# Up projection of a ConvGLU layer: token combinations of the second half made early and kept in DRAM, and boundary pairs in a new product order

## The chip, the cores and the metric

The kernel runs on one core of one Trainium2 chip. The metric is device time in microseconds (us), the median of several runs.

## The reference

One layer of a hybrid encoder in float32, 2048 tokens of width 1024. After an attention and mLSTM mixer come the two lines that this change touches:

```
def conv_glu_ffn(h, w_gate, conv_w, conv_b, w_up, w_down):
    a = dwconv_centred(h @ w_gate, conv_w, conv_b)
    return (jax.nn.gelu(a, approximate=False) * (h @ w_up)) @ w_down
...
        h = rmsnorm(x, ln_ffn_g[i])
        x = x + conv_glu_ffn(h, w_ffn_gate[i], ffn_conv_w[i], ffn_conv_b[i], w_ffn_up[i], w_ffn_down[i])
```

The hidden width is 2816, so gate and up together are 2048 x 1024 by 1024 x 5632. The convolution has width 3 over the tokens.

## The kernel before, in words

**Products.** Both projections run as Strassen's algorithm on 2 x 2 blocks: seven products instead of eight, each of a combination of two weight blocks with a combination of two token blocks. Every operand is split into a high part of reduced precision (`h`, made by ScalarE's copy) and the rest (`l`, made by VectorE's subtraction), and a product is the sum of three matmuls (h h, h l, l h). With four steps of 128 along the contraction, one product of one pair is a block of 12 matmuls of 128 x 512 (lines L1811, L1812, L1813 in `matmuls`). `PRODUCTS[j]` names the weight blocks and the token blocks of product j. Products 2 and 5 use one token block as it is, the other five a sum or difference of two.

**Order.** `FfnUp` takes two passes s, one for each half of the tokens (1024). In a pass it goes through 11 pairs i of 128-feature tiles, in a pair first the gate (m = 0), then up (m = 1), and in each the seven products in `ORDER` = (1, 2, 5, 3, 4, 6, 7). That is 2 x 11 x 2 x 7 = 308 blocks, 3696 matmuls. The blocks stand in one loop over n. Block n also calls for the weight combination of block n + 3 (`AHEAD_W`; tiles `fw`, from `fraw`, L175 and L176), for the weight load of a later group (`prefetch`), and for what is due behind the finished products: `outputs` moves banks of PSUM into `ext` (gate) and `up` (L1830 copies on ScalarE, L1833 additions on VectorE), `convolve` and `product` make the result, which goes to `a_d` in DRAM. GpSimd takes some of the weight sums and the last multiplication.

**Token combinations.** The seven pairs `bh`, `bl` of a half (2 x 1 MB each) stay in memory during the whole pass, 14 of the 22 pages of the pool that all large tiles share. `tokens(s)` loads the four blocks of the half from the transposed input `xT_d` (`bx`, 1 MB each, SP's queue) and makes them, step by step. For the first half the generator `early` lets four steps run in the last steps of the mix output (`MixOut`, the stage before, one token tile of 128 in each step t), which yields products 1, 2 and 5; the other four come during the first gate. For the second half all of it happens in the up blocks of the last pair of the first pass and the blocks behind: when product j has been used for the last time, its pages go back (`del self.b[j]`) and the next step of `tokens(1)` runs.

**Ends.** Behind the last step of MixOut stands the last tile's normalisation (`xn`, L1658), its eight transposes on TensorE and the store of `xT` to `xT_d` (L1737, ScalarE's queue); `next(between)` places the transposes and the store at block 2. `begin` clears the borders of `ext` (L1854, L1855), which uses slots of the small pool `raw` (four) that also holds `xT`, `xn` and early sums. At the other end, during the up blocks of the last pair, `next(after)` runs steps of `FfnDown.first`, which makes the first weights (`wd`, from `dr`) of the down projection and its first token sums (`as`, `al`, in `combine`, from `ar`); its matmuls are lines L147 to L149. `combine` takes the `al` tile from `slot`, a ring of four of which the first loads hold some.

Of the kernel before, what the change touches and what calls it, by code (L numbers as in the profile page):

```python
# [1755 lines left out]
class FfnUp(Strassen):  # L1756
# [5 lines left out]

    def __init__(self, g, pool):
# [7 lines left out]
        self.w, self.raws = {}, {}  # L1771
        self.blocks = [(s, i, m, j) for s in range(2) for i in range(NF // 2) for m in range(2) for j in ORDER]
# [13 lines left out]
    def weights(self, n):  # L1786
# [3 lines left out]
        if n % 7 == 0:  # L1790
            self.r = self.raws.pop(n // 7)
# [4 lines left out]
        def blk(x):  # L1796
            return None if x is None else self.r[:, 4 * x[1]:4 * x[1] + 4, P * x[0]:P * x[0] + P]

        one, two, sign = PRODUCTS[j][0]
        total = None if two is None else self.total([P, 4, P], n < NRAW)  # L1800
        split_sum(g, [nc.gpsimd if on_pool(j, e) else nc.vector for e in range(2)], w[:, 0], w[:, 1], blk(one), blk(two), sign, total)
        self.w[n] = w
        if n % 7 == 6:
            self.r = None
# [9 lines left out]

    def prefetch(self, q):

        if q < len(self.blocks) // 7:
            s, i, m, _ = self.blocks[7 * q]
            self.raws[q] = self.load_w(i, m)

    def run(self, between, after, tokens):
# [3 lines left out]
        st = Ctx()  # L1825

        def outputs(bank, dst):
# [7 lines left out]
            (c11, c12), (c21, c22) = dst  # L1835
            return {
# [55 lines left out]

        for n in range(AHEAD_W):
            if n not in self.w:
                self.weights(n)
        acts = {}
        for n in range(N + 1):
            if n < N:
                s, i, m, j = self.blocks[n]
                if j == 1:  # L1900
                    bank = {}
                    ext = up = dst = steps = None
                    dst = begin(s, i, m)
                    steps = outputs(bank, dst)
                    self.prefetch(n // 7 + 2)
# [24 lines left out]
            if j in steps:  # L1930
                todo.append(steps[j])
# [406 lines left out]
```

## Time and profile before

| what | value |
| --- | --- |
| median of 3 runs | 3026.34 us (3025.4 to 3026.8) |
| the profiled execution, own time | 3035.82 us |
| its span | 3034.1 us |
| mean granted TensorE clock over the span | 0.959 |
| up projection in the trace | about 1421 to 2345 us |
| pass boundary | about 1877 us |

Times in the trace are microseconds from the start of the span. Engines are PE (matmul), PEld (weight load), DVE (VectorE), ACT (ScalarE), POOL (GpSimd) and SP (the queue of most DMAs). A line `A <- B: x, n, y` of a waits view says that instructions of A stood idle x us in all, n times, the longest y, until B released them.

### The profile page before, as it was taken

The page shows a single profiled execution, that of the slowest core. Times are in us where ns is not written, and L with a number is a line of the kernel's source. Part 1 is how long each engine was busy: PE and PEld are TensorE (multiplying, and loading weights), DVE is VectorE, ACT ScalarE, POOL GpSimd, SP SyncE. Part 2 cuts the span into 40 slices and gives each one's busy share as a digit, 9 for nine tenths or more (in the row PEclk, how much of TensorE's full clock was granted, in tenths as well). Part 3 has the DMA queues.
Part 4 walks back from the last instruction along what each step waited for, and adds up shares of the span by engine and source line. Part 5 has one row for each costly group of instructions (what it writes and reads, how often), then busy time and mean ns, then how long its engine had stood idle before and what let it go on. Part 6 is the DMA issues. An engine that isn't in the chain of part 4 may idle for free. (4 is left out here: it accounts for less than half of the span.)

```text
span 3034.1 us, 40809 instructions
## 1 busy us (share of the span) xinstructions
PE 2867.8 (95%) x14474; PEld 2438.3 (80%) x14474; DVE 2039.0 (67%) x4107; ACT 1277.5 (42%) x2428; POOL 1090.6 (36%) x1146
## 2 busy tenths in 40 slices
PE   8898899889999988998899999799999999999999
PEld 7877888689999877787688887688887788888887
DVE  5866796675565578435977777977777576655444
ACT  5555465424333346323444444444444332233332
POOL 2133422415554555101433333433334251452221
PEclk9999999888899999999899999899999999999999
DMA  7744425466453473666122223222224877674111
GB/s 216 213 139 132 137 88 169 120 156 132 106 128 76 145 238 120 164 208 197 58 82 84 84 84 112 69 84 84 84 83 130 301 283 245 241 258 153 44 44 44
DMA packets 378731, 419.75 MB, mean 138 GB/s; under 512 B 106560, under 2 KB 299968, under 8 KB 372880
## 3 DMA queue, kind: packets, MB, share of 16 engines
q1 hardware_dynamic: 333920, 379.40, 40.7%
q10 hardware_dynamic: 44608, 37.76, 4.0%
q8 instruction: 114, 1.87, 0.3%
q14 instruction: 89, 0.73, 0.1%
HBM read 308.16 MB, written 104.61 MB: 136 GB/s over the span
## 5 line engine op out<-in xcount | busy, mean ns | idle before, releaser
L1811 PE MATMUL ps<-bh,fw 128*128 128x512 f32 x1232 | 495.6, 403 | 33.1 <-ACT fw L176 11.4
L1813 PE MATMUL ps<-bh,fw 128*128 128x512 f32 x1232 | 491.7, 399 | 6.8 <-DVE fw L176 6.8
L1812 PE MATMUL ps<-bl,fw 128*128 128x512 f32 x1232 | 492.6, 400 | 5.6 <-DVE bl L176 3.0
L175 POOL TENSOR_TENSOR sum<-fraw 128x512 f32<-128x512 f32 x132 | 197.3, 1496 | 404.4 <-DVE fw L176 364.4
L1811 PEld LDWEIGHTS ps<-bh,fw 128*128 128x128 f32 x1232 | 236.2, 192 | 97.6 <-ACT fw L176 13.6
L1813 PEld LDWEIGHTS ps<-bh,fw 128*128 128x128 f32 x1232 | 236.0, 192 | 64.0 <-DVE fw L176 9.5
L1812 PEld LDWEIGHTS ps<-bl,fw 128*128 128x128 f32 x1232 | 236.5, 192 | 61.6 <-DVE bl L176 6.2
L148 PE MATMUL ps<-wd,as 128*128 128x512 f32 x616 | 243.3, 395 | 0.0
L147 PE MATMUL ps<-wd,as 128*128 128x512 f32 x616 | 243.2, 395 | 0.0
L176 ACT ACTIVATE fw<-sum 128x512 fp32r<-128x512 f32 x220 | 134.7, 628 | 243.1 <-DVE sum L175 142.6
L176 DVE TENSOR_TENSOR fw<-sum,fw 128x512 fp32r<-128x512 f32 x220 | 214.6, 990 | 12.0 <-ACT fw L176 11.8
L996 ACT ACTIVATE e<-psb 128x512 f32<-128x512 f32 (+2 forms) x240 | 95.6, 437 | 217.9 <-PE psb L992 206.6
L930 POOL TENSOR_SCALAR_AFFINE_SELECT e<-e 128x64 f32<-128x64 f32 (+2 forms) x225 | 103.2, 459 | 203.6 <-ACT e L996 201.9
L1884 POOL TENSOR_TENSOR act<-act,up 128x512 f32<-128x512 f32 x88 | 128.9, 1465 | 93.7 <-DVE up L1833 73.3
L958 DVE CUSTOM_DVE_ANT_0 junk<-psa,mask 128x256 bf16<-128x256 f32 (+1 forms) x304 | 111.5, 367 | 73.4 <-PE psa L950 64.4
L176 ACT ACTIVATE as<-ar 128x640 fp32r<-128x640 f32 x112 | 84.2, 785 | 160.5 <-POOL ar L175 67.1
L1875 DVE SCALAR_TENSOR_TENSOR act<-ext,fcw,act 128x512 f32<-128x512 f32 (+1 forms) x176 | 138.6, 826 | 16.7 <-ACT act L1873 15.3
L175 POOL TENSOR_TENSOR ar<-ar 128x640 f32<-128x640 f32 x40 | 72.7, 1817 | 204.7 <-DMA ar<-a_d 195.2
L147 PE MATMUL ps<-wv,bh 128*128 128x260 f32 x448 | 131.3, 293 | 9.8 <-DVE acc L439 8.4
L149 PE MATMUL ps<-wd,al 128*128 128x512 f32 x336 | 133.1, 396 | 5.6 <-DVE al L176 5.6
L147 PEld LDWEIGHTS ps<-wd,as 128*128 128x128 f32 x616 | 116.2, 189 | 27.4
L148 PEld LDWEIGHTS ps<-wd,as 128*128 128x128 f32 x616 | 116.3, 189 | 27.2
(361 smaller groups left out, 7910.5 us busy)
## 6 DMA issues: line engine op xcount, KB each, us to landing
ar<-a_d SPq DMA_DIRECT2D x56, 704.0 KB
wdr<-in_w_ffn_down_dram SPq DMA_DIRECT2D x50, 512.0 KB
fraw<-in_w_ffn_gate_dram SPq DMA_DIRECT2D x22, 1024.0 KB
fraw<-in_w_ffn_up_dram SPq DMA_DIRECT2D x22, 1024.0 KB
a_d<-act SPq DMA_DIRECT2D x88, 256.0 KB
xT_d<-xT ACTq DMA_DIRECT2D x32, 512.0 KB
bx<-xT_d SPq DMA_DIRECT2D x16, 1024.0 KB
ab<-a_d SPq DMA_DIRECT2D x40, 384.0 KB
```

The source lines that it names most:

```text
L147: g.nc.tensor.matmul(out, lhsT=sh, rhs=mh, start=start, stop=False)
L148: g.nc.tensor.matmul(out, lhsT=sh, rhs=ml, start=False, stop=False)
L149: g.nc.tensor.matmul(out, lhsT=sl, rhs=mh, start=False, stop=stop)
L175: eng[0].tensor_tensor(src, a, b, ALU.add if sign > 0 else ALU.subtract)
L176: return (lambda: g.nc.scalar.activation(hi, src, AF.Copy)), (lambda: eng[1].tensor_tensor(lo, src, hi.bitcast(F32), ALU.subtract))
L930: nc.gpsimd.affine_select(l, l, pat + [[s, half - off]], ALU.is_ge, 0.0, base=s * off + w, channel_multiplier=-1)
L958: nc.vector.tensor_tensor_reduce(shape3(p, junk[:, :n], lo, hi), o, m, 1.0, -3e38, ALU.add, ALU.max, mst[:, p, i:i + 1])
L1811: nc.tensor.matmul(ps, lhsT=w[:, 0, k], rhs=h[:, k], start=start and k == 0, stop=False, skip_group_check=True)
L1812: nc.tensor.matmul(ps, lhsT=w[:, 0, k], rhs=l[:, k], start=False, stop=False, skip_group_check=True)
L1813: nc.tensor.matmul(ps, lhsT=w[:, 1, k], rhs=h[:, k], start=False, stop=k == 3, skip_group_check=True)
L1875: nc.vector.scalar_tensor_tensor(act, ext[a][:, lo + k:hi + k], self.cw[:, k, f:f + 1], act, ALU.mult, ALU.add)
L1884: nc.gpsimd.tensor_tensor(act, act, up[a][:, lo:hi], ALU.mult)
```

## The change

- `ahead` makes the combinations of products 1, 5, 4 and 7 of the first half in the last steps of MixOut, all on VectorE, from loads of 512 KB (`bq`). `rest` makes 3, 2 and 6 in the first pair, from three loads `bx`.
- The first and the last pair of each pass (`BOTH`) run the order `ORDER2`, and alternate gate and up for each product, so that a combination is used by two blocks in a row. Their outputs are moved in another order (`PAIRED`, and a second table in `outputs`; not shown below).
- `spill` makes all seven combinations of the second half during pairs 1 to 9 of the first pass, one k of four at a time: a load `sx` of 1 MB, 12 sums and differences of VectorE and 7 copies of ScalarE, and four stores of `sp` to a new DRAM tensor `b_d`. It is one call on every second block, 13 calls for one k.
- `fetch` loads the finished combinations from `b_d` into `bh` and `bl`, two loads of 1 MB for each product, when the pages of the first half come free. `tokens(1)` is gone.
- `next(after)` is still called in the up blocks of the last pair, which now alternate with the gate's. `combine` takes a page for the `al` tile of the down projection's first three items.

```
+    ORDER2 = (1, 5, 4, 7, 3, 2, 6)
+    BOTH = ((0, 0), (0, NF // 2 - 1), (1, 0), (1, NF // 2 - 1))
+    COME = (0, 2, 3, 4, 5, 6, 7, 8)
+    LOADS = (7, 9)
...
+        self.groups = [(s, i, m) for s in range(2) for i in range(NF // 2) for m in range(2)]
+        self.blocks = []
+        for s in range(2):
+            for i in range(NF // 2):
+                pair = [(s, i, m, j) for m in range(2) for j in ORDER]
+                self.blocks += sorted(pair, key=lambda b: self.ORDER2.index(b[3])) if (s, i) in self.BOTH else pair
...
+    def ahead(self):
+        g, nc = self.g, self.g.nc
+        parts = [(j, k) for j in self.ORDER2[:4] for k in (0, 2)]
...
+            r = page(g, [P, 2, 2, 512], F32, name="bq")
+            for q, blk in enumerate((one, two)):
+                if blk is not None:
+                    nc.sync.dma_start(r[:, q], self.block(0, *blk, k, 2))
+            raws.append(r)
...
+        for n, (j, k) in enumerate(parts):
+            two, sign = PRODUCTS[j][1][1:]
+            r = raws.pop(0)
+            h, l = self.pages(j) if k == 0 else self.b[j]
+            for q in range(2):
+                a = r[:, 0, q]
+                split_sum(g, (nc.vector, nc.vector), h[:, k + q], l[:, k + q], a, None if two is None else r[:, 1, q], sign, a)
+            r = None
+            if n + 2 < len(parts):
+                load(*parts[n + 2])
+            yield
...
+    def rest(self):
+        g, nc = self.g, self.g.nc
+        blocks = {}
+        def load(*blk):
+            blocks[blk] = page(g, [P, 4, 512], F32, name="bx")
+            nc.sync.dma_start(blocks[blk], self.block(0, *blk))
...
+        load(0, 1)
+        load(1, 1)
+        yield
+        load(0, 0)
+        yield
+        yield from make(3)
+        blocks.pop((1, 1))
+        yield from make(2)
+        yield from make(6)
...
+    def spill(self):
+        g, nc = self.g, self.g.nc
+        x = g.xT.rearrange("(r k p) n -> p r k n", r=2, p=P)
+        for k in range(4):
+            r = page(g, [P, 2, 1024], F32, name="sx")
+            nc.sync.dma_start(r, x[:, :, k, S // 2:])
+            yield
+            yield
+            def blk(b):
+                return None if b is None else r[:, b[0], 512 * b[1]:512 * b[1] + 512]
+            for n, j in enumerate(ORDER):
+                if n % 2 == 0:
+                    o = page(g, [P, 2, 2, 512], F32R, name="sp")
+                one, two, sign = PRODUCTS[j][1]
+                h, l = o[:, n % 2, 0], o[:, n % 2, 1]
+                split_sum(g, (nc.vector, nc.vector), h, l, blk(one), blk(two), sign, l.bitcast(F32))
+                yield
+                if n % 2 or n == 6:
+                    n0 = n - n % 2
+                    nc.sync.dma_start(g.bd[n0:n + 1, :, k].rearrange("j p q n -> p j q n"), o[:, :n + 1 - n0].bitcast(F32))
+                    o = h = l = None
+                    yield
+            r = None
+    def fetch(self, j):
+        for q, r in enumerate(self.pages(j)):
+            self.g.nc.sync.dma_start(r.bitcast(F32), self.g.bd[ORDER.index(j), :, :, q])
...
+        spilled = self.spill()
...
-                if m == i == 0:
+                if s == i == 0 and b in self.COME:
                     next(tokens, None)
+                if s == 0 and 0 < i and not both and n % 2 == 0:
+                    next(spilled, None)
+                if s == 0 and i == NF // 2 - 1 and b == 0:
+                    for _ in spilled:
+                        pass
                 t = {6: 1, 7: 4}.get(j, j)
                 if t == j:
-                    bank[j] = psum(g)
-                self.matmuls(n, bank[t], t == j)
-                if m == 1 and i == NF // 2 - 1:
-                    del self.b[j]
-                    if s == 0:
-                        if j == ORDER[0]:
-                            tokens = self.tokens(1)
-                        next(tokens)
-                    else:
-                        next(after, None)
+                    bank[m][j] = psum(g)
+                self.matmuls(n, bank[m][t], t == j)
+                if i == NF // 2 - 1:
+                    if m == 1:
+                        del self.b[j]
+                        if s == 0:
+                            gone.append(j)
+                        else:
+                            next(after, None)
+                if gone and m == 0:
+                    self.fetch(gone.pop())
...
+    def end(self, dtype, name):
+        return page(self.g, [P, 6, P], dtype, name=name)
...
-                self.combine(n + 1, slot)
+                self.combine(n + 1, slot if n > 1 else self.end)
...
-            tokens = up.tokens(0)
+            ahead, tokens = up.ahead(), up.rest()
             def early():
-                for _ in range(10):
+                for _ in range(9):
                     yield
-                for _ in range(4):
-                    next(tokens)
+                next(ahead)
+                yield
+                for x in range(4):
+                    next(ahead)
+                    next(ahead)
+                    if x == 3:
+                        up.prefetch(0)
                     yield
-                up.prefetch(0)
                 up.prefetch(1)
                 yield
                 up.weights(0)
-                yield
                 up.weights(1)
...
+    g.bd = dram.tile([7, P, 4, 2, 512], F32, name="b_d")
```

VectorE, in order of the program, from the last steps of the mix output to the first blocks of the up projection. `ss` and `xn` belong to the last token tile's normalisation, `fw` and its `sum` to weights, `bl` and `bx` to token combinations, `ext` to the gate's output, and the MEMSETs clear its borders. Before:

```order
L175 TENSOR_TENSOR sum<-fraw 128x512 x2
L1656 TENSOR_SCALAR ss<-ss 128x1
L1658 SCALAR_TENSOR_TENSOR xn<-xt,rstd,gffn 128x1024
L176 TENSOR_TENSOR fw<-sum,fw 128x512 x2
L1854 MEMSET ext 128x1
L1855 MEMSET ext 128x1
L1854 MEMSET ext 128x1
L1855 MEMSET ext 128x1
L176 TENSOR_TENSOR fw<-fraw,fw 128x512 x2
L175 TENSOR_TENSOR sum<-bx 128x512
L1833 TENSOR_TENSOR ext<-ext,ps 128x512
L176 TENSOR_TENSOR bl<-sum,bh 128x512 x2
```

Of the change, at the same place:

```order
L176 TENSOR_TENSOR fw<-sum,fw 128x512
L1656 TENSOR_SCALAR ss<-ss 128x1
L1978 MEMSET ext 128x1
L1979 MEMSET ext 128x1
L1978 MEMSET ext 128x1
L1979 MEMSET ext 128x1
L1658 SCALAR_TENSOR_TENSOR xn<-xt,rstd,gffn 128x1024
L176 TENSOR_TENSOR fw<-sum,fw 128x512
L175 TENSOR_TENSOR sum<-fraw 128x512
L176 TENSOR_TENSOR fw<-sum,fw 128x512
L176 TENSOR_TENSOR fw<-fraw,fw 128x512 x2
L175 TENSOR_TENSOR bx<-bx 128x512
```

The MEMSETs have moved ahead of the last tile's `xn`; before, they stood behind it.

SP's queue at the pass boundary: `a_d` are stores of results, `fraw` loads of weights, `bx` loads of token blocks, and `bh` and `bl` the new loads of finished combinations. Before:

```order
L1891 DMA a_d<-act 128x4x128 x3
L1783 DMA fraw<-in_w_ffn_up_dram 128x8x256
L1891 DMA a_d<-act 128x4x128
L220 DMA bx<-xT_d 128x4x512 x4
L1891 DMA a_d<-act 128x4x128 x3
L1783 DMA fraw<-in_w_ffn_gate_dram 128x8x256
L1891 DMA a_d<-act 128x4x128
L1783 DMA fraw<-in_w_ffn_up_dram 128x8x256
L1891 DMA a_d<-act 128x4x128
L1783 DMA fraw<-in_w_ffn_gate_dram 128x8x256
```

Of the change:

```order
L1894 DMA fraw<-in_w_ffn_up_dram 128x8x256
L2015 DMA a_d<-act 128x4x128
L1883 DMA bh<-b_d 128x4x512
L2015 DMA a_d<-act 128x4x128
L1883 DMA bl<-b_d 128x4x512
L2015 DMA a_d<-act 128x4x128 x3
L1883 DMA bh<-b_d 128x4x512
L1883 DMA bl<-b_d 128x4x512
L1883 DMA bh<-b_d 128x4x512
L1883 DMA bl<-b_d 128x4x512
L1894 DMA fraw<-in_w_ffn_gate_dram 128x8x256
L1883 DMA bh<-b_d 128x4x512
```

Four loads of token blocks went, and fourteen of combinations came (seven of these stand in the rows), from earlier in the last pair on.

VectorE in one pair of the first pass that is no boundary pair; L1833 and L1947 are the same addition of a PSUM bank. Before:

```order
L1854 MEMSET ext 128x1
L1855 MEMSET ext 128x1
L1833 TENSOR_TENSOR up<-up,ps 128x512
L176 TENSOR_TENSOR fw<-fraw,fw 128x512 x2
L1833 TENSOR_TENSOR ext<-ext,ps 128x512
L176 TENSOR_TENSOR fw<-sum,fw 128x512 x2
L175 TENSOR_TENSOR sum<-fraw 128x512
```

Of the change, with `sp` the combinations of the second half:

```order
L176 TENSOR_TENSOR fw<-sum,fw 128x512
L175 TENSOR_TENSOR sum<-fraw 128x512
L1947 TENSOR_TENSOR up<-up,ps 128x512
L175 TENSOR_TENSOR sp<-sx 128x512
L175 TENSOR_TENSOR sum<-fraw 128x512
L176 TENSOR_TENSOR sp<-sp 128x512
L176 TENSOR_TENSOR fw<-sum,fw 128x512 x2
L176 TENSOR_TENSOR fw<-fraw,fw 128x512 x2
L1947 TENSOR_TENSOR ext<-ext,ps 128x512 x3
```

A sum and a low part of the second half's combinations have come between the weights' instructions; some of these calls make a low part alone.

## Rows read from the trace of the kernel before

**Rows 1.** Page, section 1: busy time by engine over the span.

```profile
PE 2867.8 (95%) x14474; PEld 2438.3 (80%) x14474; DVE 2039.0 (67%) x4107; ACT 1277.5 (42%) x2428; POOL 1090.6 (36%) x1146
```

**Rows 2.** Windows: length, busy PE, PEld, DVE, ACT, POOL, PE clock, DMA share, GB/s.

```profile
1421.00:1526.00 105.00, 86.41 (x321) 64.27 (x322) 87.47 (x122) 50.30 (x86) 43.59 (x29) 0.85 0.30 93
1526.00:1870.00 344.00, 344.00 (x1481) 277.23 (x1480) 263.95 (x399) 153.06 (x257) 126.07 (x85) 1.00 0.28 86
1870.00:1982.00 112.00, 89.83 (x338) 69.28 (x337) 103.12 (x141) 54.32 (x95) 53.68 (x34) 0.88 0.26 82
1982.00:2335.00 353.00, 353.00 (x1532) 286.80 (x1531) 264.03 (x409) 161.20 (x273) 133.69 (x92) 1.00 0.29 88
2335.00:2372.00 37.00, 27.57 (x101) 21.58 (x100) 24.59 (x29) 11.29 (x19) 15.41 (x11) 0.82 0.69 211
```

**Rows 3.** Waits, 1421 to 1466 us: total, times, longest.

```profile
PEld ps L1811 <- ACT bh L176: 9.9, 5, 5.0
...
ACT ext L1830 <- DMA xT_d<-xT: 7.6, 1, 7.6
...
PE ps L1811 <- ACT bh L176: 6.9, 3, 4.6
...
DVE ext L1854 <- DMA xT_d<-xT: 5.5, 1, 5.5
```

**Rows 4.** Waits, 1500 to 1526 us.

```profile
PE ps L1811 <- DVE ext L1833: 5.5, 1, 5.5
```

**Rows 5.** Waits, 1870 to 1930 us.

```profile
PE ps L1811 <- ACT fw L176: 10.1, 4, 6.6
...
PE ps L1813 <- DVE fw L176: 6.8, 4, 3.1
```

**Rows 6.** Waits, 2335 to 2372 us.

```profile
PE ps L149 <- DVE al L176: 5.6, 1, 5.6
DVE al L176 <- DMA a_d<-edge: 5.4, 1, 5.4
...
PEld ps L1811 <- ACT wd L176: 4.2, 1, 4.2
...
PE ps L1811 <- DVE up L1833: 3.8, 1, 3.8
```

**Rows 7.** Lines, DVE by form, 1526 to 1838 us: count, busy us, mean ns, idle before.

```profile
L176 DVE TENSOR_TENSOR fw<-sum,fw 128x512 fp32r<-128x512 f32 x80 | 84.3, 1070 | 2.5 <-ACT fw L176 2.5
...
L175 DVE TENSOR_TENSOR sum<-fraw 128x512 f32<-128x512 f32 x32 | 35.9, 1122 | 0.3
...
L1833 DVE TENSOR_TENSOR ext<-ext,ps 128x512 f32<-128x512 f32 x48 | 32.0, 681 | 5.6 <-ACT ext L1830 3.3 <-PE ps L1813 2.3
```

**Rows 8.** Tile bx, whole span: duration ns min/median/max, first and last start.

```profile
L176 DVE TENSOR_TENSOR bl<-bx,bh x60: 674/681/1786, 94.5 to 1922.2; 128x512 fp32r<-128x512 f32 x60
...
L175 DVE TENSOR_TENSOR sum<-bx x18: 676/680/1786, 1371.6 to 1907.9; 128x512 f32<-128x512 f32 x18
...
L175 POOL TENSOR_TENSOR bx<-bx x8: 1261/1592/1779, 366.5 to 1894.7; 128x512 f32<-128x512 f32 x8
```

**Rows 9.** Timeline, DVE, 1419 to 1438 us: start, duration, engine, line, idle before.

```profile
1422.81 0.15 DVE L1656 TENSOR_SCALAR ss<-ss 128x1 f32<-128x1 f32 x1
1423.69 1.28 DVE L1658 SCALAR_TENSOR_TENSOR xn<-xt,rstd,gffn 128x1024 f32<-128x1024 f32 x1 [0.73 <-POOL rstd L1657]
...
1431.66 0.06 DVE L1854 MEMSET ext<- 128x1 f32 x1 [5.49 <-DMA xT_d<-xT]
```

**Rows 10.** Timeline, ACT, same stretch.

```profile
1420.48 0.44 ACTq L1737 DMA_DIRECT2D xT_d<-xT  x1
```

**Rows 11.** Windows around one stall; columns as in Rows 2.

```profile
1499.06:1507.54 8.48, 2.93 (x13) 2.06 (x11) 8.29 (x12) 2.33 (x4) 3.25 (x3) 0.79 0.10 36
1507.54:1511.90 4.36, 4.36 (x13) 3.46 (x13) 3.28 (x5) 1.15 (x2) 2.22 (x2) 0.63 0.02 4
1511.90:1514.69 2.79, 2.79 (x14) 2.26 (x12) 1.80 (x3) 1.87 (x3) 0.23 (x1) 1.00 0.00 0
```

**Rows 12.** Windows; three steady pairs of 39 us.

```profile
1526.00:1565.00 39.00, 39.00 (x169) 31.40 (x168) 30.41 (x47) 17.84 (x30) 14.71 (x11) 1.00 0.26 81
1565.00:1604.00 39.00, 39.00 (x170) 31.49 (x169) 30.60 (x47) 17.84 (x30) 14.89 (x11) 1.00 0.26 82
```

**Rows 13.** Windows in the mix output, where before makes its first combinations.

```profile
1356.00:1366.00 10.00, 10.00 (x49) 8.24 (x48) 2.12 (x3) 2.77 (x6) 0.54 (x1) 1.00 1.04 343
1366.00:1376.00 10.00, 10.00 (x49) 8.22 (x48) 7.81 (x9) 3.82 (x7) 2.73 (x2) 1.00 0.44 150
...
1396.00:1406.00 10.00, 10.00 (x45) 8.12 (x44) 3.33 (x5) 2.69 (x6) 0.54 (x1) 1.00 1.00 316
```

**Rows 14.** Windows at the pass boundary and at the start of the down projection.

```profile
1890.00:1900.00 10.00, 4.93 (x22) 3.69 (x20) 9.85 (x12) 3.56 (x7) 8.17 (x5) 0.99 0.52 157
2370.00:2380.00 10.00, 10.00 (x43) 8.12 (x42) 2.95 (x5) 1.47 (x2) 0.00 (x0) 0.95 1.02 422
```

More of the change, by code (lines that the diff above doesn't have):

```diff
@@ new lines, in block, with pages, load @@
+    def block(self, s, kr, tc, k0=0, n=4):
+        x = self.g.xT.rearrange("(k p) n -> p k n", p=P)
+        c0 = 512 * (2 * s + tc)
+        return x[:, 4 * kr + k0:4 * kr + k0 + n, c0:c0 + 512]
+    def pages(self, j):
+        self.b[j] = [page(self.g, [P, 4, 512], F32R, name=name) for name in ("bh", "bl")]
+        return self.b[j]
+    def ahead(self):
+        g, nc = self.g, self.g.nc
+        parts = [(j, k) for j in self.ORDER2[:4] for k in (0, 2)]
+        raws = []
+        def load(j, k):
+            one, two, _ = PRODUCTS[j][1]
+            r = page(g, [P, 2, 2, 512], F32, name="bq")
[3 more added lines that the diff above has]
+            raws.append(r)
+        load(*parts[0])
+        load(*parts[1])
+        yield
[10 more added lines that the diff above has]
+            yield
@@ new lines, in rest, with make @@
+    def rest(self):
[4 more added lines that the diff above has]
+            nc.sync.dma_start(blocks[blk], self.block(0, *blk))
+        def make(j):
+            one, two, sign = PRODUCTS[j][1]
+            a, b = blocks[one], None if two is None else blocks[two]
+            h, l = self.pages(j)
+            for ks in ((0, 2), (1, 3)):
+                for k in ks:
+                    eng = [nc.gpsimd if k in on else nc.vector for on in TPOOL]
+                    split_sum(g, eng, h[:, k], l[:, k], a[:, k], *((None, 0, None) if b is None else (b[:, k], sign, b[:, k])))
+                yield
[8 more added lines that the diff above has]
+        yield from make(6)
@@ L1899, in run @@
                 s, i, m, j = self.blocks[n]
+                both = (s, i) in self.BOTH
+                q = self.groups.index((s, i, 0 if both else m))
+                b = 2 * self.ORDER2.index(j) + m if both else ORDER.index(j)
                 if j == 1:
[L1901 to L1905, printed above, removed]
+                    bank[m] = {}
+                    steps[m] = None
+                    ext = up = None
+                    steps[m] = outputs(bank[m], begin(s, i, m), both)
+                for x in ([q + 2 + self.LOADS.index(b)] if b in self.LOADS else []) if both else [q + 2] if b == 0 else []:
+                    self.prefetch(x)
                 if n + AHEAD_W < N:
@@ L2041, in piece @@
             return half(1024).rearrange("p (f a) n -> p f (a n)", f=2)
-        def end(dtype, name):
-            return page(g, [P, 6, P], dtype, name=name)
         for n in range(3):
-            self.load(n, end)
+            self.load(n, self.end)
         ws = self.weights(self.ORDER[0], piece, (g.nc.gpsimd, g.nc.vector))
@@ L2050, in first @@
         yield
[L2051 removed]
+        self.combine(0, self.end)
         next(ws)
```

67 lines of the change are left out of this document (43 added, 24 removed).

## The prediction

> **What bounds the kernel now.** I read the page first: TensorE is busy for 2867.8 of 3034.1 us, VectorE for 2039.0 [rows 1]. So TensorE is the bound over most of the span, and a change can only give back time in which it waits or runs at the lower clock. The change touches the up projection and its two ends, so next I cut that stage into windows [rows 2]. In two long stretches TensorE is busy all the time at clock 1.00: 344 + 353 us for 1481 + 1532 instructions, or 0.2313 us for each. At this rate the other three stretches would need 321 x 0.2313 = 74.2, 338 x 0.2313 = 78.2 and 101 x 0.2313 = 23.4 us. They take 105, 112 and 37. What is lost is 30.8 us at the start, 33.8 at the pass boundary and 13.6 at the end: **78.2 us, the ceiling of any gain here** as long as the number of matmuls stays, which it does.
>
> Then the waits, to see what ends last in each. At the start TensorE waits for token combinations (ScalarE's `bh`) while ScalarE and VectorE stand behind a store of `xT` for 7.6 and 5.5 us [rows 3], and later once for VectorE's addition to `ext`, 5.5 us [rows 4]: VectorE is 87.47 of 105 us busy there, and behind. At the boundary VectorE is the bound, 103.12 of 112 us [rows 2], and TensorE waits for weights that VectorE and ScalarE make late [rows 5]. At the end TensorE waits 3.8 us for VectorE's addition and 5.6 us for `al`, which waits for the store of `edge` [rows 6]. So nearly all of the loss is token work, or the first work of the down projection, put on VectorE while TensorE already runs.
>
> A stall costs more than its own length. The block with a stall took 8.48 us and the next 4.36 at a granted clock of 0.63, against 2.79 at 1.00 for the third [rows 11]. So behind a stall of some 5.7 us come 1.6 us that are lost to the clock.
>
> **The start.** Four of the seven combinations move into the mix output, 28 VectorE instructions (three with a sum and a low part for four k, one with low parts alone) where before had products 1, 2 and 5. At the median of 0.68 us [rows 8] the 28 are 19 us over some five steps. There TensorE is 10.00 of 10 us busy while VectorE has at most 7.81, mostly less [rows 13], so they fit. Three combinations stay for the first pair, and each is now used by two blocks in a row, so that the fifth combination is needed at block 8 and no longer at block 4. Counted from the order of instructions, VectorE's large operations of the first pair fall from 62 to 49. With a tenth for the other work beside them this is about the length of a pair, and VectorE stays a few us ahead.
>
> One thing gets worse. Of the change, the MEMSETs that clear `ext` stand ahead of the last tile's `xn`. In the trace the MEMSET waited until 1431.66 for a store of `xT` issued at 1420.48, and `xn` had run at 1423.69 [rows 9, 10]. Now `xn` waits too, and behind it the eight transposes, placed at block 2, and all of TensorE's later work. Two blocks end at 1421.0 + 24 x 0.2313 = 1426.6; `xn` is ready at 1431.7 + 1.3 = 1433.0. That is a stall of 6.4 us, then 1.6 us of low clock. If the store lands sooner, this shrinks. I take 6.4 + 1.6 and 1 for small waits: 9 us are left of 30.8, a **gain of 22** (5 to 26: the lower end if VectorE still falls behind as in rows 4, the upper if the store is quick).
>
> **The boundary.** The sums and lows for the second half, 38 on VectorE and ten on GpSimd, leave the boundary. Fourteen loads of 1 MB come instead, 14.7 MB, issued from the second block of the last pair on, as pages come free. The last combinations are used some 72 us later (a pair and most of the next: 26 blocks of 2.78 us), so 14.7 / 72 = 204 GB/s are needed, and 86 beside them for weights and results [rows 2]: 290 in all. Rows at this kernel's loads show 316 to 422 GB/s while TensorE runs at 1.00 or nearly [rows 13, 14]. At the boundary itself 157 were moved at half of the DMA share [rows 14], which is what was asked for and no limit. The first pair to use them comes one pair (38.9 us) after its pages were freed. VectorE then has the load of a steady pair, 30.5 of 39 us [rows 12]. I leave 1.3 us of loss: a **gain of 32.5** (33.8 at most; 27 if one load is late by two blocks).
>
> **The end.** The up blocks of the last pair, at which the first work of the down projection is called, are now spread over 14 blocks, so VectorE and GpSimd have twice the time for `dr` and `wd`, and `al` has a page and need not wait for the store of `edge`. I leave 1.6 of 13.6: a **gain of 12** (3 to 13; the lower end if `wd` is merely late elsewhere, for the DMA engines are 0.69 busy there [rows 2]).
>
> **What it costs.** The spill adds 48 VectorE instructions, 28 copies on ScalarE, 4 MB of loads and 14.7 MB of stores. It makes 52 calls, 7 in each pair, over 7.4 pairs or 289 us. VectorE is free for 39 - 30.5 us of 39 [rows 12], so 63 us in that time. The 48 cost 33 us at 0.68 and 52 at the 1.07 to 1.12 us that two-input instructions on weights average beside GpSimd [rows 7]. Both fit. At the longest row, 1.79 us [rows 8], they are 86 us, 23 too many. I take the middle one, since GpSimd works on in these pairs, and nothing on the path. ScalarE is 17.8 of 39 us busy [rows 12] and covers 28 short copies; the 18.7 MB in 289 us are 65 GB/s beside 86. For weights that come a little late, and for the loads in the mix output (0.5 MB each, where the DMA engines are full at times [rows 13]), I take 2.5 us, and 0 to 26 as the bounds.
>
> A row speaks against the spill: the same operation with a PSUM input takes 0.681 us, with two SBUF inputs 1.070 [rows 7]. The Trainium skill, "GPSIMD Engine Reference", Specifications, says that GpSimd shares its SBUF interfaces with VectorE, and that VectorE's instructions with two SBUF inputs contend. All 48 added ones are of this kind; by that rule none comes at 0.68 while GpSimd is busy, and where each waits out a whole GpSimd instruction the second rival below is the result. The trace agrees as far as the means go.
>
> **Sum.** 22 + 32.5 + 12 - 2.5 = 64 us. The profiled execution took 3035.82 us of its own, so it would take 2971.8. It stands 9.5 us above the median of the runs, 3026.34, so the median becomes **2962 us**.
>
> **The rivals.**
> 1. *VectorE falls behind at the start after all* (0.15). It starts the first pair late behind the MEMSET, with 49 operations for a pair; at the 1.07 us of two-input instructions they alone are 52 us. For: 87.47 of 105 us busy before, and the wait for `ext` only in the second pair. Against: fewer operations, and a weaker demand per block. Start loss 25 and not 9: 2962 + 16 = 2978.
> 2. *VectorE becomes the bound in the first pass* (0.12). Each added instruction waits out a GpSimd instruction (1.59 us at the median, 1.79 at the longest [rows 8]): 86 - 63 = 23 us, 2985. For: the long rows. Against: the means.
> 3. *The end is not recovered* (0.10): the first loads of the down projection come late, and all 13.6 us stay: 2962 + 12 = 2974.
> 4. *The fetch is late* (0.05). TensorE then stands at the boundary for what is missing. The gain elsewhere is 32 us; with the 32 of the boundary lost as well the kernel is as before, so lateness of 64 us decides: 14.7 MB in 72 + 64 us, 108 GB/s. Below it the kernel is slower: at 100 GB/s 147 us, 75 late, **3037**. For: 157 GB/s in all at the boundary, 86 of which would go to other loads. Against: 316 to 422 elsewhere.
> That the change does nothing (a new wait of the same size at each place) gets 0.02.
>
> **How the numbers follow.** The forecast has 0.56: with its own bounds 2948 (the ceiling of 78 us) to 2978. The range has to take in the first three rivals, and a fetch that is some us late: 2948 to 2992. It leaves out rival 4's far side and two rivals together. A difference below 0.2% (6 us) is about what a measurement of this kernel can't tell from no change. All cases but rival 4 and the last are faster by more: 0.93, within 0.02, slower 0.05.
>
> **What would show it.** In the changed profile: TensorE at 1.00 and without waits through the pass boundary; one stall of 5 to 7 us behind the second block, ended by `xn` or the MEMSET's store; VectorE at 36 to 38 of 39 us in pairs 1 to 8, and TensorE full there; loads of `bh` and `bl` that land before their blocks. The prediction is wrong if TensorE waits for `fw` in the first pass (VectorE is the bound), for `bh` or `bl` at the boundary (the fetch), if the mix output's steps grow beyond their length of before, or if stalls at the start only move to the second pair.

## The result

The changed kernel takes 2990.87 us (median of 4 runs, 2988.41 to 2994.65), the kernel before 3026.57 us beside it. The ratio is 0.988, 95% interval 0.9868 to 0.9893: 35.7 us faster. Forecast were 2962 us and a range of 2948 to 2992. So the direction is right and the time lies at the range's far end, 1.1 us inside it: little more than half of the 64 us came.

I cut both traces at the same blocks: 0 to 13 (pair 0), 14 to 27 (pair 1), 28 to 139 (pairs 2 to 9), 140 to 153 (pair 10), 154 to 181 (pairs 11 and 12), 182 to 293, 294 to 307 (the last pair), and the first 100 matmuls of the down projection. Windows, columns as in [rows 2]. Before: blocks 0 to 27, 28 to 139, 140 to 181, and the last pair with those matmuls:

```profile
1421.02:1531.59 110.57, 92.00 (x345) 68.50 (x345) 93.04 (x130) 52.17 (x89) 46.66 (x31) 0.86 0.29 92
1531.59:1844.04 312.45, 312.45 (x1345) 251.92 (x1344) 244.38 (x370) 142.78 (x240) 118.22 (x80) 1.00 0.27 81
1844.04:1994.95 150.91, 128.74 (x505) 100.80 (x504) 127.26 (x178) 68.42 (x118) 63.07 (x41) 0.91 0.29 91
2304.88:2380.79 75.91, 66.48 (x269) 53.21 (x268) 42.95 (x59) 24.58 (x40) 26.05 (x17) 0.91 0.71 233
```

The changed kernel, all stretches but blocks 182 to 293:

```profile
1422.37:1471.83 49.46, 42.43 (x176) 34.13 (x177) 35.48 (x52) 24.56 (x44) 18.26 (x12) 0.93 0.40 134
1471.83:1521.51 49.68, 42.05 (x169) 32.58 (x168) 44.81 (x70) 24.78 (x42) 21.94 (x15) 0.93 0.43 147
1521.51:1846.41 324.90, 314.03 (x1345) 255.01 (x1344) 269.88 (x416) 152.78 (x265) 120.54 (x81) 0.98 0.40 131
1846.41:1884.97 38.56, 38.56 (x169) 31.55 (x168) 23.98 (x36) 13.61 (x23) 11.50 (x8) 1.00 0.92 332
1884.97:1966.02 81.05, 78.41 (x337) 62.79 (x336) 67.46 (x103) 41.18 (x70) 31.42 (x23) 1.00 0.39 127
2276.39:2317.54 41.15, 39.04 (x168) 31.11 (x167) 29.68 (x33) 18.67 (x33) 22.73 (x16) 1.00 0.57 196
2317.54:2340.82 23.28, 23.28 (x102) 18.97 (x101) 17.81 (x25) 7.75 (x12) 4.84 (x4) 1.00 0.67 180
```

The lengths in us, and what the prediction had for them; the first row is the end of the mix output, the last 300 matmuls ahead of block 0:

| stretch | before | after | difference | predicted |
| --- | --- | --- | --- | --- |
| end of the mix output | 65.03 | 69.27 | +4.2 | in the 2.5 |
| blocks 0 to 27, the start | 110.57 | 99.14 | -11.4 | -22 |
| blocks 28 to 139, the spill | 312.45 | 324.90 | +12.5 | +2.5, all costs |
| blocks 140 to 181, the boundary | 150.91 | 119.61 | -31.3 | -32.5 |
| blocks 182 to 293 | 309.93 | 310.37 | +0.4 | 0 |
| last pair and first 100 down matmuls | 75.91 | 64.43 | -11.5 | -12 |

Without the first row the sum is 41.3 us; with what lies ahead (1422.37 for 1421.02) and behind it is the difference of the two spans, 3034.1 and 2992.9. The boundary and the end came as forecast. TensorE is busy in all of pair 10, while 332 GB/s are moved at 0.92 of the DMA engines. The start gave half, and pairs 2 to 9, which had no loss, have one of 12 us.

The mix output has grown, which the start of block 0 alone does not show (windows of the 300 matmuls, before and after, then waits in the second):

```profile
1355.99:1421.02 65.03, 63.77 (x302) 52.19 (x300) 31.47 (x44) 23.35 (x43) 6.70 (x8) 1.00 0.65 209
```

```profile
1353.10:1422.37 69.27, 64.97 (x302) 52.09 (x300) 36.77 (x57) 26.23 (x50) 5.58 (x7) 1.00 0.77 252
```

```profile
ACT mts L142 <- DMA mraw<-mt_d: 32.8, 5, 8.1
...
PE ps L147 <- ACT mts L142: 3.1, 2, 1.8
```

TensorE waits for `mts`, which ScalarE makes from a load; that load now stands among those of `bq`. The same wait of ScalarE was 14.4 us before, and TensorE had none for `mts`.

At the start, the MEMSET waits as foreseen, here for a store issued at 1421.83 (timelines of VectorE and of ScalarE):

```profile
1433.93 0.06 DVE L1978 MEMSET ext<- 128x1 f32 x1 [9.49 <-DMA xT_d<-xT]
...
1434.11 1.28 DVE L1658 SCALAR_TENSOR_TENSOR xn<-xt,rstd,gffn 128x1024 f32<-128x1024 f32 x1
```

```profile
1421.83 0.41 ACTq L1737 DMA_DIRECT2D xT_d<-xT  x1
```

The `xn` behind it starts at 1434.11, and TensorE stands: the stall, 8.8 us beyond a block's usual length, was put at 6.4. But then pair 1 takes 49.68 us where a pair takes 38.6, with VectorE busy 44.81. What VectorE does there (lines, count, busy us and mean ns):

```profile
L1999 DVE SCALAR_TENSOR_TENSOR act<-ext,fcw,act 128x512 f32<-128x512 f32 x11 | 9.8, 925 | 0.7 <-ACT act L1997 0.7
L1947 DVE TENSOR_TENSOR ext<-ext,ps 128x512 f32<-128x512 f32 x9 | 5.9, 678 | 1.9 <-PE ps L1923 1.9
...
L1947 DVE TENSOR_TENSOR up<-up,ps 128x512 f32<-128x512 f32 x8 | 5.3, 680 | 0.5 <-PE ps L1923 0.5
```

A pair has 12 additions of banks and 8 instructions of the convolution. Here are 17 and 11: VectorE still works off pair 0. In both pairs together it is busy for 80.3 us, more than the 77.7 us that their 336 matmuls take at the rate of [rows 2].

In pairs 2 to 9 TensorE stalls at four places, behind blocks 61, 82, 89 and 117. One of them, the end of block 89 (waits, then VectorE's timeline, then windows of the stall and of the next block):

```profile
PE ps L1921 <- DVE ext L1947: 4.0, 1, 4.0
```

```profile
1694.14 1.29 DVE L176 TENSOR_TENSOR fw<-fraw,fw 128x512 fp32r<-128x512 f32 x2 [2.95 <-ACT fw L176]
...
1697.21 1.28 DVE L176 TENSOR_TENSOR fw<-sum,fw 128x512 fp32r<-128x512 f32 x2
1698.53 1.64 DVE L175 TENSOR_TENSOR sum<-fraw 128x512 f32<-128x512 f32 x1
1700.09 1.27 DVE L1947 TENSOR_TENSOR ext<-ext,ps 128x512 f32<-128x512 f32 x2
```

```profile
1696.40:1700.82 4.42, 0.44 (x2) 0.01 (x1) 4.38 (x8) 1.17 (x2) 1.65 (x1) 0.88 0.74 234
1700.82:1706.10 5.28, 5.28 (x12) 4.13 (x13) 2.42 (x5) 0.01 (x1) 1.60 (x1) 0.50 0.01 2
```

VectorE stood 3.0 us for ScalarE, then took its queue in order: low parts, additions, weights again, and only at 1700.09 the addition that reads product 4's bank. Block 90 (product 7) adds onto that bank and could not start before. The next block then ran at 0.50, the lower of the clock's two levels, for 5.28 us.

What each instruction of the spill costs on VectorE (lines by form, 1521 to 1846 us), and who waited for the stores to `b_d` in the whole span (tile view: us, times):

```profile
L176 DVE TENSOR_TENSOR sp<-sp 128x512 fp32r<-128x512 f32 x18 | 16.8, 936 | 2.4 <-ACT sp L176 2.3
L175 DVE TENSOR_TENSOR sp<-sx 128x512 f32<-128x512 f32 x18 | 15.9, 892 | 0.2
L176 DVE TENSOR_TENSOR sp<-sx,sp 128x512 fp32r<-128x512 f32 x6 | 6.3, 1047 | 0.0
```

```profile
  ACT fw L176: 18.0, 4
```

Their means of 892 to 1047 ns lie between the 680 and the 1070 to 1122 of [rows 7]. A mean mixes short and long ones here (tile `sp`, whole span, ns min/median/max):

```profile
L175 DVE TENSOR_TENSOR sp<-sx x20: 676/681/1792, 1489.9 to 1764.0; 128x512 f32<-128x512 f32 x20
```

The view of `b_d` shows a wait that the prediction did not have: ScalarE's `fw` takes a page from which `sp` is still being stored.

### The profile page after: what moved, and what is told of

Its sections match the earlier page's. It is cut to its first block, busy times and chain, and to the rows that moved or that the text cites. A ratio compares the mean times of both kernels' runs of the same rounds, so it can differ in the third digit from the quotient of the medians.

```text
span 2992.9 us, 40910 instructions
## 1 busy us (share of the span) xinstructions
PE 2837.8 (95%) x14474; PEld 2421.4 (81%) x14474; DVE 2022.8 (68%) x4122; ACT 1272.5 (43%) x2428; POOL 1065.4 (36%) x1131
## 4 chain that ended last, share of the span: by engine, by line
PE 47%; DVE 6%; DMA 2%; ACT 2%; issue 2%; POOL 1%; SPq 0%; POOLq 0%; DVEq 0%; ACTq 0%
PE ps L149 8%; PE ps L147 8%; PE ps L148 8%; PE ps L1921 7%; PE ps L1923 7%; PE ps L1922 6%; DVE fw L176 2%; DMA mraw<-mt_d 1%; DVE act L1999 1%; DVE sum L175 1%; ACT fw L176 1%; DVE ext L1947 1%; PE ps L2284 1%; DVE up L1947 0%; POOL sum L175 0%
## 5 line engine op out<-in xcount | busy, mean ns | idle before, releaser
L1921 PE MATMUL ps<-bh,fw 128*128 128x512 f32 x1232 | 489.3, 397 | 20.6 <-DVE ext L1947 14.0
L1923 PE MATMUL ps<-bh,fw 128*128 128x512 f32 x1232 | 486.0, 395 | 3.9 <-DVE fw L176 3.9
L1922 PE MATMUL ps<-bl,fw 128*128 128x512 f32 x1232 | 485.4, 394 | 0.0
L1921 PEld LDWEIGHTS ps<-bh,fw 128*128 128x128 f32 x1232 | 233.4, 189 | 78.6 <-DVE ext L1947 11.3
L1923 PEld LDWEIGHTS ps<-bh,fw 128*128 128x128 f32 x1232 | 232.8, 189 | 60.2 <-DVE fw L176 6.6
L176 DVE TENSOR_TENSOR fw<-sum,fw 128x512 fp32r<-128x512 f32 x220 | 195.0, 901 | 25.4 <-ACT fw L176 24.5
L2008 POOL TENSOR_TENSOR act<-act,up 128x512 f32<-128x512 f32 (+1 forms) x88 | 125.3, 1426 | 129.2 <-DVE up L1947 73.1
L147 PE MATMUL ps<-wv,bh 128*128 128x260 f32 x448 | 131.1, 293 | 9.1 <-DVE acc L439 5.2
L148 PE MATMUL ps<-wv,bh 128*128 128x260 f32 x448 | 130.5, 291 | 3.8 <-DVE wv L176 3.8
```

The costliest lines, as they stand in the source:

```text
L147: g.nc.tensor.matmul(out, lhsT=sh, rhs=mh, start=start, stop=False)
L148: g.nc.tensor.matmul(out, lhsT=sh, rhs=ml, start=False, stop=False)
L176: return (lambda: g.nc.scalar.activation(hi, src, AF.Copy)), (lambda: eng[1].tensor_tensor(lo, src, hi.bitcast(F32), ALU.subtract))
L1921: nc.tensor.matmul(ps, lhsT=w[:, 0, k], rhs=h[:, k], start=start and k == 0, stop=False, skip_group_check=True)
L1922: nc.tensor.matmul(ps, lhsT=w[:, 0, k], rhs=l[:, k], start=False, stop=False, skip_group_check=True)
L1923: nc.tensor.matmul(ps, lhsT=w[:, 1, k], rhs=h[:, k], start=False, stop=k == 3, skip_group_check=True)
```

## The experiments

The theories were these. For pairs 2 to 9: *pages* (the wait for the store just named), *VectorE full* (48 instructions more than it can take), and *latency* (VectorE has time enough, but is in order, and once in a while late with the one addition that product 7 needs). For the start: the MEMSET's wait, the spill's first steps in pair 1, or a VectorE that carries pair 0 into pair 1.

The runs stood on several chips, where the kernel before took 3030.2 to 3032.2 us, so ratios to it are compared, and stretches of the profiles.

**The spill without its arithmetic.** Out go `split_sum` and the `sp` page, and the store reads a page of the first half:

```
-                    o = page(g, [P, 2, 2, 512], F32R, name="sp")
-                split_sum(g, (nc.vector, nc.vector), h, l, blk(one), blk(two), sign, l.bitcast(F32))
...
-                    nc.sync.dma_start(g.bd[...], o[:, :n + 1 - n0].bitcast(F32))
+                    nc.sync.dma_start(g.bd[...], self.b[1][0].rearrange(...)[:, :n + 1 - n0].bitcast(F32))
```

> Leaves out the spill's 48 sums and low parts, its 28 copies and its sp pages; the stores to DRAM keep their number and size but take another page's content, so the second half is computed from other data. The changed kernel loses 49.7 + 324.9 us for blocks 14 to 139 against 126 x 2.76 = 347.8, so 26.8 us. Both theories (page: fw takes a page from which sp is still being stored; VectorE: 48 more instructions fill its queue) expect the stalls behind block 19 to be gone, about 20 us, 2971. If what is lost in pair 1 is only a late VectorE from pair 0, blocks 14 to 27 stay near 46 us as before the change and it is 15 us, 2976.

Ratio 0.9849 (0.9835 to 0.9864). Windows of pair 1 and of pairs 2 to 9:

```profile
1473.84:1524.59 50.75, 41.74 (x170) 32.09 (x168) 46.61 (x71) 24.94 (x42) 23.76 (x16) 0.93 0.44 141
1524.59:1836.40 311.81, 311.09 (x1346) 251.81 (x1345) 241.38 (x369) 140.24 (x237) 118.27 (x81) 1.00 0.31 95
```

Pairs 2 to 9 are whole again, 13.1 us faster, pair 1 is not. So pair 1's loss is not the spill's arithmetic. By the ratios the run gains some 9 us, less than either theory had. One thing more differs than was meant: with no `sp` to wait for, all 16 stores go out from 1351.6 to 1489.9 us, in the mix output and pairs 0 and 1, for 1494.7 to 1767.9 in the changed kernel. So pairs 2 to 9 have lost the stores' traffic too (95 GB/s for 131), and pair 0, with 51.96 us, has it on top. This run alone does not part the arithmetic from the traffic; the next does.

**Only the store changed.** The arithmetic and the `sp` pages stay, the store reads the other page (the last line above). Here too the 16 stores go out early, from 1347.2 to 1483.2 us.

> Keeps the spill's sums, copies and sp pages, but stores another page's content to DRAM, so no sp page waits for its store (the second half is computed from other data). Page theory: ScalarE's waits for b_d<-sp (4.4 us in pair 1, 13.6 in pairs 2 to 9) go, and with them the stalls at blocks 19, 89 and 117, some 15 to 18 us: 2974. VectorE theory: the waits go, the stalls stay elsewhere: 2988 to 2991.

Ratio 0.9897 (0.988 to 0.9913), no gain. The profiled execution is the fastest of the four, 8.4 us under their median.

```profile
1467.65:1518.87 51.22, 43.82 (x170) 33.84 (x169) 48.00 (x72) 24.54 (x42) 23.15 (x15) 0.90 0.45 144
1518.87:1841.52 322.65, 314.64 (x1345) 254.94 (x1344) 272.08 (x415) 153.58 (x265) 123.90 (x81) 0.98 0.29 92
```

The waits of `fw` for `b_d` are gone, and so is the stores' traffic in pairs 2 to 9 (92 GB/s), and only 2.2 of the 13 us with them; the stalls behind blocks 61, 89 and 117 are still there. *Pages* falls as the main cause, the traffic too; what is left is the arithmetic, with the pages that it holds.

**Product 4 before product 3.** In the pairs that are no boundary pairs the order is (1, 2, 5, 4, 3, 6, 7):

```
+    ORDER1 = (1, 2, 5, 4, 3, 6, 7)
...
-                pair = [(s, i, m, j) for m in range(2) for j in ORDER]
+                pair = [(s, i, m, j) for m in range(2) for j in self.ORDER1]
```

> In the pairs that are no boundary pairs product 4 runs before product 3, so that product 7, which adds onto product 4's bank, comes three blocks behind it and not two; everything else is kept. Theory (latency: VectorE is not full, but once in a while more than a block late with the one addition that must empty the bank before product 7 starts, at positions 5 and 12 of a pair): blocks 28 to 139 fall from 325 to 311 to 314 us and blocks 14 to 27 from 49.7 to 44 to 46, 2970 to 2976. Rival (VectorE is the bound there): the stalls move to waits for fw, the sum stays, 2987 to 2992.

Ratio 0.982 (0.9798 to 0.9842), the largest gain of one edit.

```profile
1469.10:1516.38 47.28, 41.53 (x170) 32.24 (x168) 44.88 (x69) 24.53 (x42) 21.48 (x15) 0.96 0.43 144
1516.38:1829.65 313.27, 310.45 (x1345) 252.10 (x1344) 262.12 (x413) 151.86 (x264) 124.47 (x81) 1.00 0.42 138
```

Pairs 2 to 9 fall by 11.6 us. VectorE runs the same instructions (x413 for x416) in a shorter time and is still idle for 51 us of it. So it was not full: *VectorE full* falls, and *latency* is what the run bears out. How much of the gain comes from the instructions themselves, which took 262.12 us for 269.88, is not parted from it. Pair 1 gains 2.4 us only.

**More slack still.** The orders (1, 2, 4, 5, 3, 6, 7) and, in boundary pairs, (1, 4, 5, 7, 3, 2, 6).

> Only the two orders differ from the changed kernel: (1, 2, 4, 5, 3, 6, 7) in the steady pairs, so that product 7 comes four blocks behind product 4, and (1, 4, 5, 7, 3, 2, 6) in the boundary pairs, where it now has four blocks instead of two. Theory (latency at that one bank): beside the 15 us of the run with product 4 before product 3, the rest of the stalls at positions 5 and 12 go: blocks 28 to 139 take 310 to 311 us, the last pair 39 to 40 and not 41.2, the stall in the middle of pair 1 shrinks: 2966 to 2972. If VectorE or the pages are the limit in what is left, it stays at 2974 to 2977.

Ratio 0.9837 (0.982 to 0.9854), and pairs 2 to 9 take 319.1 us, not 310 to 311: the theory missed, and one block of distance more gave less than product 4 before 3 alone. Pair 1 falls to 43.9 us, but not by the distance alone: in this run the MEMSETs do not wait either, and `xn` starts 2.5 us behind the start of block 0 and not 11.7. Its stall at block 90 (waits, 1688 to 1695 us):

```profile
PE ps L1922 <- DVE ext L1948: 3.0, 1, 3.0
ACT fw L176 <- DMA b_d<-sp: 2.6, 1, 2.6
```

Here the addition stands in VectorE's queue behind low parts of `fw`, which wait for ScalarE, which waits 2.6 us for the store: both causes in one chain. Distance between the products alone does not do it; where the addition stands in the queue does too. How much each is worth is left open.

**The first gate's `ext` in pages.**

```
-                st.ext = [raw(g, [P, 1027], name="ext") for _ in range(2)]
+                st.ext = [(page if s == i == 0 else raw)(g, [P, 1027], name="ext") for _ in range(2)]
```

> The first gate's ext takes two pages of the large pool, so that its MEMSETs no longer wait for the store of xT, and xn behind them comes 9.5 us earlier. Theory (the MEMSET's wait is the whole stall): the 8.8 us stall at block 1 and 1.6 us of low clock go, 2980 to 2982. Rival (the same slots hold up next, for which ScalarE then waits, or VectorE is late with weights a few blocks on): a stall of the same size at blocks 3 to 8, 2988 to 2991.

Ratio 0.9862 (0.9847 to 0.9877); its interval still overlaps the change's, and it stands between theory and rival. Windows of pairs 0 and 1, and waits of 1418 to 1450 us:

```profile
1418.43:1466.35 47.92, 43.56 (x177) 34.26 (x178) 40.24 (x58) 26.57 (x46) 18.75 (x13) 0.93 0.45 144
1466.35:1511.09 44.74, 40.64 (x169) 32.60 (x168) 40.20 (x65) 22.75 (x39) 19.29 (x13) 0.96 0.47 158
```

```profile
ACT xT L1736 <- DMA xT_d<-xT: 4.6, 1, 4.6
...
PE ps L1921 <- ACT ext L1944: 4.1, 1, 4.1
```

The stall at block 1 shrinks to 1 us, but ScalarE's copy to `xT` now waits 4.6 us for a slot of the same pool, and TensorE 4.1 us at block 5 for ScalarE's copy of product 4's bank. Pair 1, with an earlier VectorE, falls from 49.7 to 44.7.

**The loads of the first pair behind the store.** `rest` issues its loads from ScalarE's queue, where the store of `xT` stands ahead of them:

```
-            nc.sync.dma_start(blocks[blk], self.block(0, *blk))
+            nc.scalar.dma_start(blocks[blk], self.block(0, *blk))
```

> The three loads of token blocks in the first pair go to ScalarE's queue, behind the store of xT that the MEMSETs wait for, and no longer beside it from SP's. Theory (that store lands 12 us after its issue because 3 MB are loaded at the same time): it lands by 1426, the stall at block 1 falls from 8.8 us to under 3, blocks 0 to 13 take 41 to 43 us and not 49.5, and the second pair falls to 45 or less as in the run with ext in pages: 2976 to 2981. Rival (the combinations of products 3, 2 and 6 are now late, or the wait moves to another slot): blocks 0 to 13 stay at 47 or more.

Ratio 0.9872 (0.9853 to 0.989), as the change. ScalarE's store, VectorE's MEMSET, the wait for the loads, and the two pairs:

```profile
1424.90 0.37 ACTq L1737 DMA_DIRECT2D xT_d<-xT  x1
```

```profile
1428.86 0.06 DVE L1978 MEMSET ext<- 128x1 f32 x1 [1.35 <-DMA xT_d<-xT]
```

```profile
DVE bx L175 <- DMA bx<-xT_d: 4.2, 1, 4.2
```

```profile
1425.44:1471.73 46.29, 43.08 (x177) 34.26 (x177) 39.76 (x56) 26.03 (x46) 18.29 (x13) 0.93 0.44 143
1471.73:1520.63 48.90, 40.83 (x169) 32.89 (x168) 43.58 (x67) 22.67 (x39) 22.68 (x14) 0.90 0.49 161
```

The store lands within 4 us, as the theory had it. But the loads, now issued later, hold VectorE up for 4.2 us, and in pair 1 TensorE waits 8.1 us for an addition at block 19. The stall moved; the rival was nearer.

**The spill from pair 2 on.**

```
-                if s == 0 and 0 < i and not both and n % 2 == 0:
+                if s == 0 and 1 < i and not both and n % 2 == 0:
```

> The spill begins in pair 2 and not in pair 1; its 52 calls then end in pair 9. If pair 1 loses its 11 us to the spill's first steps, blocks 14 to 27 take 40 to 42 us and no 49.7: 2982. If pair 0 hands a late VectorE on, as before the change (46.4 us without any spill), blocks 14 to 27 stay at 45 or more: 2987 to 2991.

Ratio 0.9878 (0.9863 to 0.9893), no difference, and in pair 1 VectorE is as busy as with the spill:

```profile
1471.74:1522.19 50.45, 42.10 (x170) 32.56 (x168) 43.66 (x65) 23.30 (x40) 24.11 (x15) 0.93 0.37 115
```

So with the spill away pair 1 stays, and with an earlier VectorE (`ext` in pages) it shrinks, as VectorE then does 40.24 us of its work in pair 0 and not 35.48. That speaks for pair 0's backlog. So does the run on slack: with an early `xn` and 13 additions in pair 1, as with `ext` in pages, and not 17, it takes 43.9 us. But the run with the loads behind the store has 14 and takes 48.9, and no run takes the backlog alone away: its share is not shown.

**The end, part by part.** The ring of four for `al` again (`self.combine(n + 1, slot)`), and the last pair in the old order (`BOTH` without its last entry), a single execution each.

> The down projection's al tiles come from the ring of four again, as before the change. If the page is what removed the wait for the store of edge, the first 100 matmuls of the down projection take 30 to 31 us again and not 23.3, 7 us more. If calling the first work over 14 blocks did it, they stay at 23.3.

> The last pair of the second pass runs in the old order, gate first and then up, so the first work of the down projection is called in seven blocks and not over fourteen. If spreading gave the gain of the last pair, its blocks take 44 to 45 us as before the change and not 41.2; the first 100 matmuls behind stay at 23.3. If the spread gave nothing, 41 or less, since the two stalls at the alternating products (1.2 and 1.7 us) go.

In the first of the two runs the last pair stays at 41.26 us. Its window of the first 100 down matmuls, TensorE's longest wait there (waits, 2342 to 2380 us), and for the second run the windows of the last pair and of those matmuls:

```profile
2325.14:2358.64 33.50, 25.16 (x102) 20.05 (x101) 20.55 (x30) 9.24 (x14) 5.29 (x4) 0.90 0.79 250
```

```profile
PE ps L149 <- DVE al L176: 8.3, 1, 8.3
```

```profile
2282.85:2323.24 40.39, 38.78 (x169) 31.26 (x168) 24.23 (x37) 15.99 (x27) 16.54 (x12) 1.00 0.68 223
2323.24:2349.83 26.59, 24.36 (x103) 18.59 (x101) 12.57 (x17) 7.44 (x11) 7.85 (x6) 1.00 0.65 169
```

Without the page these matmuls take 33.5 us for 23.28: the page is worth 10 us. Without the alternation the two stretches take 67.0 us together for 64.4: 2.6 us, and not in the last pair, where I had put them. Together this is more than the 11.5 us of both, so the two overlap, and each rests on one profile.

**The kernel before, once more.**

> The kernel before once more, for a second profile of it: the prediction took off 9.5 us because its profiled execution stood that far above its median. If that belongs to the profile or to the kernel, this one takes 3034 to 3038 again; if it is chance in the stretch ahead of the mix output, which took 1249 to 1265 us in ten profiles of kernels that are the same there, it may lie anywhere from 3024 to 3040, and the up projection takes 929 us as before.

It took 3029.99 us of its own, and 1415.9 us to the first block of the up projection, 5.1 less than in the first profile. The stretches of the up projection are the same within 0.3 us, but for the last pair and what follows:

```profile
2299.55:2339.92 40.37, 38.79 (x169) 31.28 (x167) 24.11 (x37) 16.01 (x27) 16.69 (x12) 1.00 0.68 223
2339.92:2374.99 35.07, 26.64 (x102) 19.94 (x101) 16.41 (x23) 8.79 (x13) 7.34 (x6) 0.90 0.76 245
```

They are 40.37 + 35.07 = 75.4 us here for 75.9: in these two profiles chance decides only in which of the two the wait falls. In all 14 profiles the time to the first block lies between 1415.9 and 1430.0 us. The end of the mix output in it is no chance: its 300 matmuls take 65.0 us in both profiles of before and 69.3 to 73.7 in the twelve with the change, most in the two runs whose stores to `b_d` fall there too (72.7 and 73.7). Up to there it is 1344.5 to 1360.3 us, without relation to the edits.

**All edits together.** `ext` in pages, the spill from pair 2 on and both orders of the run on slack; then the same with (1, 2, 5, 4, 3, 6, 7) in the steady pairs.

> The orders of the run before, with the first gate's ext in pages and the spill from pair 2 on. If pair 1's loss is VectorE's backlog, which the MEMSET's wait and the spill's first steps add to, and the narrow place at product 7 turns the backlog into stalls, then blocks 0 to 27 fall from 99 us to 84 to 88: 2955 to 2962. If they only trade one stall for another, as the runs with one of these edits did (95 and 93 us), they stay at 92 or more and it is within 6 us of the run with the orders alone.

> The run with all edits, but in the steady pairs the order (1, 2, 5, 4, 3, 6, 7) of the run that gave 313 us there. Sum of the best stages so far: blocks 0 to 13 41 us, 14 to 27 45 to 46, 28 to 139 313, last pair 41: 54 to 58 us under the kernel before in the up projection, ratio 0.980 to 0.982. If the stalls in the steady pairs fall where the scheduler's order happens to put a late instruction, and not by the slack alone, blocks 28 to 139 take 316 to 320 again and the ratio stays at 0.982 to 0.984.

The first has ratio 0.9818 (0.9803 to 0.9832), with 87.0 us for blocks 0 to 27, as expected, but 316.9 for pairs 2 to 9; it missed its 2955 to 2962 with 2976.39. The second has 0.9813 (0.9793 to 0.9833), 2974.59 us beside 3032.18:

```profile
1423.59:1464.84 41.25, 40.52 (x176) 32.15 (x177) 35.67 (x52) 24.71 (x43) 17.82 (x12) 1.00 0.49 161
1464.84:1513.56 48.72, 42.77 (x170) 33.00 (x168) 44.18 (x68) 23.06 (x39) 21.88 (x15) 0.93 0.39 119
1513.56:1824.92 311.36, 309.52 (x1346) 252.03 (x1344) 262.07 (x416) 153.65 (x267) 124.19 (x81) 1.00 0.42 140
```

It is faster than both kernels, its interval lies clear of the change's, but not of that of the run with product 4 first alone (0.982). Pair 0 has lost its stalls, pairs 2 to 9 are at 311.4, as expected. Pair 1 is not: 48.72 us, VectorE 44.18 busy, for the 45 to 46 expected. So pair 0's stalls are not what makes pair 1 long: in the shorter pair 0 VectorE gets no more done, and pair 1 has 17 additions again. This pair is left, and the mix output.

## Why the prediction was right in direction and short in size

- **The boundary** (32.5 predicted, 31.3 measured) and **the end** (12 and 11.5) stand. Of the end the reason was named, but not its shares: taken away one at a time, the page is worth 10, the spread 2.6.
- **The start** (22 predicted, 11.4 measured). The step that failed is "VectorE stays a few us ahead". The stall behind the MEMSET was foreseen, at 8 us with the clock, and took some 10. But the operations were counted for the first pair alone. The new order makes the outputs of a pair complete late, so additions and convolutions of pair 0 fall into pair 1, and VectorE's work in the two is 80.3 us. By the rate of [rows 2] 28 blocks take 77.7 us, so 21.4 are lost and not 9; rival 1, with 0.15, had 25 and was nearer. What else has a part in pair 1's loss stays open.
- **The cost of the spill** (2.5 predicted with all else, 12.5 measured in pairs 2 to 9). The step that failed is "Both fit", with "nothing on the path". They did fit: VectorE was free for 55 of 324.9 us, and the 42 instructions in this stretch took 39.0 us, 0.93 each, less than the 1.07 to 1.12 of the sum. But the addition that product 7 needs was due within a block, and at 1700.09 it came after all that stood ahead of it in VectorE's queue; free time in the mean did not cover that. Where it stands in the queue matters beside the distance, as the run on slack shows, and the shares stay open. The new wait of `fw` for the store was not seen either; with the stores' traffic it is 2 us. Rival 2 had a price of 23 by another mechanism, a full VectorE, which the run with product 4 first speaks against, and so does the median of the spill's sums, 0.681 us: half of them took about the shortest time. Its rule stands as far as it goes: the Trainium skill, "GPSIMD Engine Reference", Specifications, has VectorE's instructions with two SBUF inputs contend with GpSimd, and the trace agrees in the means (892 to 1047 ns for the spill's, 680 for those from PSUM).
- **The loads in the mix output** were in the same 2.5 us. They cost 4.2 more, and with that one of the prediction's own signs of being wrong came: the mix output's steps grew. Another came in part: pair 1 takes 49.68 us where it took 46.43.
- **From the profile to the median.** Taking off the 9.5 us between them is the same as taking the 64 us from the median, and no error. But the spans of the two profiles differ by 41.2 us and the medians by 35.5. Chance has a part in that: the first profile of before took 5 us more up to the 300 matmuls than the second (1355.99 for 1350.91). Of the 28.5 us that are missing the start is 10.6, the spill 10.0, the mix output 4.2, the boundary 1.2 and the end 0.5; some 2 us are left, within the noise.
- **The range** held by 1.1 us, and that is luck: it left out two rivals together, and two came, each in part (the start, and the first pass by another mechanism than rival 2's).

## What to carry to other kernels

Work moved under a busy engine needs more than free time there: find the instruction on the helping engine that the busy one needs soonest, count how much may stand ahead of it in the queue, and widen that place (here the swap of two products gave back 11.6 us). When an order is changed, count the helper's work by where its results become complete, over the next stage too. When loads are moved into a busy stage, look which of its own loads they delay. When a wait is removed, look who else uses the slot: here the wait for the store of `xT` came back on ScalarE's copy. And when an experiment takes a dependency away, look in the trace where its transfers have gone.

## What the runs showed of the hardware

A store of 512 KB took 12.1 us to land (1421.83 to 1433.93) while 3 MB of loads ran from another queue, and 4.0 us (1424.90 to 1428.86) with the loads behind it in its own. The Trainium skill, "DMA: Bandwidth & Descriptors", Queues, rings and completion order, says that a DMA engine goes round between the queues it has work for, packet by packet, which agrees as far as the trace goes: the store in a queue of its own got a share, no precedence. That the turns go by packets no run here shows. And a stall of 4.4 us (1696.40 to 1700.82) was followed by a whole block at the lower clock, 5.28 us and so 2.5 more than a block takes at the rate of [rows 2].
